# Feed-forward products by one level of Strassen's algorithm, and the gated products through DRAM to a separate output stage

## The chip, the cores and the metric

The kernel runs on one core of a Trainium2 chip. The metric is device time in microseconds: the median of the runs, from the start of the execution to its end. A core has a matrix engine (TensorE; "PE" in the profile, with its weight loads as "PEld"), three engines for elementwise work (VectorE "DVE", ScalarE "ACT", GpSimd "POOL"), and queues that issue transfers (SyncE "SP" here for nearly all loads, POOL's queue for stores). The matrix engine reads the on-chip SBUF and writes the accumulator memory PSUM, of 8 banks with 512 four-byte columns each, on 128 partitions.

## The reference

One inference step of a small two-layer backbone on 1152 tokens (128 context tokens and 1024 latent tokens), model width 1024. Layer 0 mixes tokens by retention and pooling, layer 1 by attention. After each mixer comes a feed-forward block, and this is what the change is about:

```python
def swiglu(h, w_in, w_out):
    a, b = jnp.split(h @ w_in, 2, axis=-1)
    return (jax.nn.silu(a) * b) @ w_out

fs = swiglu(rmsnorm(xs, norm_gain[i, 2]) * (1.0 + sc2s) + sh2s, w_ffn_in[i], w_ffn_out[i])
xs = xs + g2s * rmsnorm(fs, norm_gain[i, 3])
```

`w_in` is 1024 x 5632 (2816 gate columns `a`, 2816 value columns `b`), `w_out` is 2816 x 1024. The same is done for the context tokens with their own shift, scale and gate. sc2, sh2 and g2 come from a modulation that multiplies silu(c) with a 1024 x 6144 matrix per layer.

## The kernel before, in words

Everything is float32. A product that must keep its precision is made of three single-pass matmuls on the reduced type `F32R`: each operand is split into a rounded high part and the residue, and hi x hi, hi x lo and lo x hi are summed in PSUM (`mm3`, line 177). `split` makes the pair: a cast on ScalarE (line 154), a subtraction on VectorE (line 155).

Tokens are 9 tiles of 128 (`NT`), in 3 groups of 384 (`NG`, `GT`). `O` holds the residual tokens' normed values token by token; `hsteps` transposes them on TensorE (line 246), applies shift and scale on ScalarE (line 249) and splits into `h_hi` and `h_lo` in the large buffer `RR` (lines 251, 252). These steps are put into a list `later`, and `go(n)` issues n of them between matmul groups.

`out_proj` is the projection at the end of a mixer, by token tile; the last two tiles hold back part of their matmuls, between which the first group of `hsteps` is issued. `chain` is the norm with residual behind a tile's projection or feed-forward output: a sum of squares on ScalarE (217), 1/sqrt on GpSimd (182, 183), gain and residual on VectorE (229, 230), a store of the residual from POOL's queue, a second sum of squares (233), and a scale (235).

`ffn` runs over 11 pairs of 128-column tiles of the 2816 columns (`NPAIR`). In a pair, `A(p, g)` makes the gate and value product of a token group: per tile, 24 matmuls of 384 columns for the gate and 24 for the value (8 row tiles of the weights x 3 passes), then Silu on ScalarE (791), a product on VectorE (792) and a split. `B(p, g)` multiplies the result with two row tiles of `w_out`: 18 groups of 6 matmuls of 512 columns a pair, each added into `O` by VectorE (816; the first pair is copied by ScalarE, 814). The loads of the next pair's weights go through two staging buffers `RAW` and are split. In layer 0's block, `hook()` issues small units of the next layer's modulation (`Ada`): a load of 512 KB, four multiply-adds on VectorE (333), and from time to time a pair of matmuls with a ones column (316).

The order of the work is that of the program; the tile framework then sets the order on each engine by priorities and by when an instruction is ready, and adds the semaphores. Loads queue on SP in that order.

## Time and profile before

| what | value |
|---|---|
| median of 3 runs | 3002.43 us (3002.17 to 3002.64) |
| profiled execution, span | 2999.9 us; its own total is not recorded beside the span |
| busy: PE, DVE, ACT, POOL | 98%, 50%, 30%, 9% of the span |
| moved by DMA | 205.18 MB, mean 68 GB/s |
| layer 0's feed-forward block | about 692 to 1565 us, layer 1's about 2156 us to the end |

A row of a group view names line, engine, operation, tiles written and read, shape and count, then busy time and mean length of one in ns, then the idle time before such instructions and what ended it. A matmul's length in the profile includes its passage through the array, so that matmuls overlap; how often they start tells what they cost. L177 is a line of `mm3`, which every split product shares; the tiles and shapes tell them apart: in the feed-forward block `PS<-RR` with 128x384 is the first product, and `PS<-MID2True,MID1True` with 128x512 the second.

### The profile page before, as it was taken

The page shows a single profiled execution, that of the slowest core. Times are in us where ns is not written, and L with a number is a line of the kernel's source. Part 1 is how long each engine was busy: PE and PEld are TensorE (multiplying, and loading weights), DVE is VectorE, ACT ScalarE, POOL GpSimd, SP SyncE. Part 2 cuts the span into 40 slices and gives each one's busy share as a digit, 9 for nine tenths or more (in the row PEclk, how much of TensorE's full clock was granted, in tenths as well). Part 3 has the DMA queues.
Part 4 walks back from the last instruction along what each step waited for, and adds up shares of the span by engine and source line. Part 5 has one row for each costly group of instructions (what it writes and reads, how often), then busy time and mean ns, then how long its engine had stood idle before and what let it go on. Part 6 is the DMA issues. An engine that isn't in the chain of part 4 may idle for free. (4 is left out here: it accounts for less than half of the span.)

```text
span 2999.9 us, 40862 instructions
## 1 busy us (share of the span) xinstructions
PE 2949.6 (98%) x16907; PEld 2659.8 (89%) x16907; DVE 1502.4 (50%) x2483; ACT 910.5 (30%) x1678; POOL 279.7 (9%) x497
## 2 busy tenths in 40 slices
PE   7999999999999999999999999999999999999998
PEld 4889998789888888999989988888899999999997
DVE  5783346436455554333375567885523333333335
ACT  5222223324211111111153467874431111111112
POOL 2010112110000000000034621110100000000001
PEclk9999999999999999999999999999999999999999
DMA  7531110413333332111131000002311111111112
GB/s 242 170 105 48 34 32 33 149 59 97 92 99 99 99 99 85 43 43 43 43 128 61 22 15 1 29 29 85 127 43 43 43 43 43 43 43 43 43 43 99
DMA packets 169396, 205.18 MB, mean 68 GB/s; under 512 B 7085, under 2 KB 126313, under 8 KB 169081
## 3 DMA queue, kind: packets, MB, share of 16 engines
q1 hardware_dynamic: 163968, 186.67, 19.8%
q0 software_dynamic: 4752, 15.52, 1.3%
q8 instruction: 132, 2.16, 0.3%
q14 instruction: 56, 0.45, 0.0%
q10 hardware_dynamic: 488, 0.38, 0.0%
HBM read 182.33 MB, written 20.22 MB: 68 GB/s over the span
## 5 line engine op out<-in xcount | busy, mean ns | idle before, releaser
L177 PE MATMUL PS<-RR 128*128 128x384 f32 (+2 forms) x10800 | 1805.9, 324 | 3.4 <-DVE O L229 1.9
L177 PEld LDWEIGHTS PS<-RR 128*128 128x128 f32 x10800 | 1717.1, 189 | 49.9 <-issue 19.0
L177 PE MATMUL PS<-MID2True,MID1True 128*128 128x512 f32 x2376 | 568.2, 396 | 0.5 <-DVE O L816 0.5
L177 PEld LDWEIGHTS PS<-MID2True,MID1True 128*128 128x128 f32 x2376 | 443.8, 188 | 109.9 <-issue 4.2
L792 DVE TENSOR_TENSOR XGT<-XGT,PS 128x384 f32<-128x384 f32 x132 | 73.1, 554 | 553.5 <-PE PS L177 551.5
L816 DVE TENSOR_TENSOR O<-PS,O 128x512 f32<-128x512 f32 x360 | 245.7, 689 | 165.3 <-PE PS L177 164.8
L155 DVE TENSOR_TENSOR RR<-RAW,RR 128x1024 fp32r<-128x1024 f32 (+1 forms) x141 | 172.8, 1230 | 232.1 <-ACT RR L154 208.8
L177 PE MATMUL PS<-RR,MID2True 128*128 128x256 f32 (+1 forms) x1464 | 280.5, 340 | 0.3 <-DVE MID2True L155 0.2
L154 ACT CAST RR<-RAW 128x1024 fp32r<-128x1024 f32 (+1 forms) x141 | 147.0, 1047 | 409.6 <-PE PS L177 389.8
L177 PEld LDWEIGHTS PS<-RR,MID2True 128*128 128x128 f32 x1464 | 226.8, 189 | 32.6 <-DVE MID2True L155 0.7
L182 POOL TENSOR_SCALAR SM<-SM 128x1 f32<-128x1 f32 (+1 forms) x153 | 56.6, 370 | 1655.0 <-ACT RR L217 1178.5
L154 ACT CAST MID1True<-XGT 128x384 fp32r<-128x384 f32 x132 | 67.6, 512 | 376.2 <-DVE XGT L792 376.1
L177 PE MATMUL PS<-MID1True,RR 128*128 128x512 f32 (+1 forms) x576 | 145.2, 369 | 2.2 <-ACT XGT L1032 1.7
L791 ACT ACTIVATE XGT<-PS 128x384 f32<-128x384 f32 x132 | 64.5, 489 | 243.1 <-PE PS L177 238.8
L333 DVE SCALAR_TENSOR_TENSOR XGT<-XGT,PW 128x512 f32<-128x512 f32 x168 | 117.3, 747 | 17.7 <-ACT XGT L331 12.3
L1030 DVE TENSOR_REDUCE SM<-PS 128x1 f32<-128x1280 f32 x64 | 95.4, 1491 | 41.6 <-PE PS L177 41.1
L154 ACT CAST RR<-PS 128x512 fp32r<-128x512 f32 x160 | 93.6, 586 | 64.0 <-PE PS L1048 62.9
L154 ACT CAST MID2True<-RAW 128x1024 fp32r<-128x1024 f32 x44 | 44.2, 1046 | 221.0 <-PE PS L177 220.7
L177 PEld LDWEIGHTS PS<-MID1True,RR 128*128 128x128 f32 x576 | 92.4, 189 | 15.4 <-ACT XGT L1032 2.6
L183 POOL TENSOR_TENSOR SM<-SM,PW 128x1 f32<-128x1 f32 (+1 forms) x153 | 103.8, 679 | 12.4
L155 DVE TENSOR_TENSOR RR<-PS,RR 128x512 fp32r<-128x512 f32 x160 | 103.8, 682 | 1.3 <-ACT RR L154 1.3
L1048 PE MATMUL PS<-CT,XGT 128*128 128x128 f32 x640 | 98.6, 276 | 0.7 <-DVE RR L155 0.7
(208 smaller groups left out, 1936.8 us busy)
## 6 DMA issues: line engine op xcount, KB each, us to landing
RAW<-in_w_ffn_in_dram SPq DMA_DIRECT2D x88, 512.0 KB
XGT<-in_w_ada_dram SPq DMA_DIRECT2D x54, 512.0 KB
RAW<-in_w_ffn_out_dram SPq DMA_DIRECT2D x44, 512.0 KB
O<-in_w_ada_dram SPq DMA_DIRECT2D x32, 512.0 KB
RAW<-in_w_in_even_dram SPq DMA_DIRECT2D x28, 512.0 KB
x<-XGT POOLq DMA_DIRECT2D x27, 512.0 KB, 3.0
XGT<-x SPq DMA_DIRECT2D x23, 512.0 KB
RAW<-in_w_out_even_dram SPq DMA_DIRECT2D x12, 512.0 KB
```

Of the source, the lines that this page charges most:

```text
L154: nc.scalar.copy(hi, src)
L155: nc.vector.tensor_sub(lo, src, hi)
L177: nc.tensor.matmul(out=out, lhsT=x, rhs=y, start=(first and c == 0), stop=(last and c == n - 1))
L182: nc.gpsimd.tensor_scalar(r, ss, 1.0 / n, EPS, op0=ALU.mult, op1=ALU.add)
L183: nc.gpsimd.tensor_tensor(r, r, nhalf[:, 0:w], op=ALU.pow)
L333: nc.vector.scalar_tensor_tensor(self.acc[kind], b[:, k], sv, self.acc[kind], op0=ALU.mult, op1=ALU.add)
L791: nc.scalar.activation(tm, pss[0], ACTF.Silu)
L792: nc.vector.tensor_mul(tm, tm, pss[1])
L816: nc.vector.tensor_add(dst, p3, dst)
L1030: nc.vector.reduce_max(nm, sp, axis=AX.X, negate=True)
L1048: nc.tensor.transpose(tp[:, c:c + 128], smx[n, e][:, j * 128:(j + 1) * 128], ident)
```

## The change

The first product is done by Strassen's algorithm in Winograd's form, one level deep: the tokens are cut into two halves of 576, the 1024 model columns into two halves of 512, and the output columns into gate and value. With X the normed tokens and A the weights of one 128-column tile f (`a11`, `a12` for the gate, `a21`, `a22` for the value), four sums of weight blocks and five sums of token blocks (three of them sums proper, and the plain second half counted in) enter seven block products P1 to P7, where the plain way has eight. Each block product is 12 matmuls over 192 token columns and 12 over 384 (`product`, line 829). `prep` splits one weight block or sum for the product three steps on; the sums are made on GpSimd (`sums`, 809). `after` takes a product from PSUM and adds it on: the first half of the tokens' gate is P1 + P2 in PSUM, the other parts are built on VectorE from u2 and u3 (858 to 871). The gated product of a tile, 128 x 1152, is stored to DRAM (`gg_scr`).

The token sums need all nine tiles. `first_half` makes the operands of P1 and P2 during the held-back matmuls of `out_proj`; `second_half` makes the rest beside eight P1 and P2 products of the first four tiles (`NPRO`), which go ahead of the loop.

The second product is a stage of its own after all 22 tiles (`output`): chunks of 2, 4, 3, 4, 2, 3, 4 tiles (`NCH`), for each of which the gated products come back from DRAM through one staging buffer (`gr`) and are split, and 18 groups of 6 matmuls per tile run; VectorE adds into `O` once a chunk. In the last chunk the norm chain of each token tile starts when the tile is done. `chain` became a generator so that its steps can be laid between others. The modulation units go to two places of the loop and of the output stage, and with `shared` they add their row right away, because their PSUM bank is also a product's.

```diff
-        def A(p, g, fs=range(2)):
-            for f in fs:
-                pss = []
-                for ab in range(2):
-                    hi, lo = (x.rearrange("p (k f) -> p k f", k=KD) for x in w_unit(2 * f + ab))
-                    ps = bank(ab if abank["n"] % 2 == 0 else 2 + ab)[:, 0:GT]
-                    mm3(ps, [(hi[:, k], lo[:, k], h_hi(g)[:, k], h_lo(g)[:, k]) for k in range(KD)])
...
+    PROD = {P1: ("a", 0, 0, 0), P6: ("s", 1, 3, 1), P7: ("s", 2, 4, 2), P5: ("s", 0, 2, 3),
+            P2: ("a", 1, 1, 0), P4: ("a", 3, 5, 2), P3: ("s", 3, 6, 3)}
+            pro = [(0, P1), (1, P1), (0, P2), (1, P2), (2, P1), (3, P1), (2, P2), (3, P2)]
+            self.steps = pro + [(f, p) for f in range(NF)
+                                for p in ((P6, P7, P5, P4, P3) if f < NPRO else (P1, P6, P7, P5, P2, P4, P3))]
...
+        def sums(self, f):
+            nc.gpsimd.tensor_tensor(s[0], a21, a22, op=ALU.add)
+            nc.gpsimd.tensor_tensor(s[1], s[0], a11, op=ALU.subtract)
+            nc.gpsimd.tensor_tensor(s[2], a11, a21, op=ALU.subtract)
+            nc.gpsimd.tensor_tensor(s[3], a12, s[1], op=ALU.subtract)
...
+        def product(self, s):
+            for c0, w, o in ((0, 192, 320), (192, 384, 512)):
+                ps = PS[:, 1024 * reg + o:1024 * reg + o + w]
+                for k in range(4):
+                    ks = slice(128 * k, 128 * k + 128)
+                    xh, xl = self.xop(x, k, 0, c0, w), self.xop(x, k, 1, c0, w)
+                    for u, v in ((wh, xh), (wh, xl), (wl, xh)):
+                        nc.tensor.matmul(out=ps, lhsT=u[:, ks], rhs=v, start=first and n == 0, stop=n == 11,
...
+        def second_half(self, j, b):
+                    nc.tensor.transpose(ps[:, i * 128:(i + 1) * 128], O[:, k, t * 128:(t + 1) * 128], ident)
+                self.evac_h(k, ps[:, p0:p0 + w], tm, ((1, 0, w),))
+            nc.vector.tensor_sub(t1, x12, op(0, 0))
+            nc.vector.tensor_sub(t1, t1, op(0, 1))
+            nc.gpsimd.tensor_tensor(t3, x22, x12, op=ALU.subtract)
+            nc.scalar.copy(op(6, 0), x22)
+            nc.scalar.copy(op(2, 0), t1)
+            nc.vector.tensor_sub(t2, x22, t1)
+            nc.scalar.copy(op(3, 0), t2)
+            nc.vector.tensor_sub(op(2, 1), t1, op(2, 0))
+            nc.vector.tensor_sub(t4, op(1, 0), t2)
+            nc.vector.tensor_add(t4, t4, op(1, 1))
+            nc.scalar.copy(op(5, 0), t4)
+            nc.scalar.copy(op(4, 0), t3)
+            nc.vector.tensor_sub(op(3, 1), t2, op(3, 0))
+            nc.vector.tensor_sub(op(5, 1), t4, op(5, 0))
+            nc.gpsimd.tensor_tensor(op(6, 1), x22, op(6, 0), op=ALU.subtract)
+            nc.gpsimd.tensor_tensor(op(4, 1), t3, op(4, 0), op=ALU.subtract)
...
+        def out_prep(self, f):
+            gh, gl, wh, wl = self.out_slot(f)
+            gr = XGT[:, 4096:5248]
+            nc.sync.dma_start(out=gr, in_=gg_scr[self.l][f])
+            w = raw()
+            nc.sync.dma_start(out=w, in_=a["w_ffn_out"][self.l, f * 128:(f + 1) * 128, :])
+            split(gh, gl, gr)
+            for h in range(2):
+                split(wh[h], wl[h], w[:, 512 * h:512 * h + 512])
...
+            for ci, nf in enumerate(NCH):
+                for t in range(NT):
+                    for half in range(2):
+                        mm3(ps, items)
+                        if ci == 0:
+                            nc.scalar.copy(dst, p3)
+                        else:
+                            nc.vector.tensor_add(dst, p3, dst)
+                        if todo and n % every == 0:
+                            self.out_prep(todo.pop(0))
```

Three places where the order of instructions differs. First TensorE at the end of layer 0's mixer and the start of its feed-forward block. Rows name line, operation, output and inputs, shape and count; L246 and, after, L891 and L910 are transposes. Before:

```order
L246 MATMUL PS<-CT,O 128x128 x3
L177 MATMUL PS<-RR,MID2True 128x512 x24
L246 MATMUL PS<-CT,O 128x128 x12
L177 MATMUL PS<-RR 128x384 x56
L246 MATMUL PS<-CT,O 128x128 x6
L177 MATMUL PS<-RR 128x384 x16
```

And after, the same place:

```order
L891 MATMUL PS<-CT,O 128x128 x4
L179 MATMUL PS<-RR,MID2True 128x512 x24
L910 MATMUL PS<-CT,O 128x128 x4
L843 MATMUL PS<-RR 128x192 x12
L843 MATMUL PS<-RR 128x384 x12
L910 MATMUL PS<-CT,O 128x128 x6
```

Where transposes of the later groups lay between long runs of 384-column matmuls, there now stand four or six transposes of `second_half` ahead of each of eight products of 12 + 12.

Second TensorE in the middle of the block. Before, a pair:

```order
L177 MATMUL PS<-RR 128x384 x96
L177 MATMUL PS<-MID2True,MID1True 128x512 x24
L316 MATMUL PS<-XGT,PW 32x512 x2
L177 MATMUL PS<-MID2True,MID1True 128x512 x48
L177 MATMUL PS<-RR 128x384 x192
```

After, from a product on plain `RR` operands to the end of an f-tile's seven (P4 reads `MID1True`, P3 `MID2True` and two blocks elsewhere):

```order
L843 MATMUL PS<-RR 128x192 x12
L843 MATMUL PS<-RR 128x384 x12
L843 MATMUL PS<-MID1True,RR 128x192 x12
L843 MATMUL PS<-MID1True,RR 128x384 x12
L843 MATMUL PS<-MID2True,RR 128x192 x10
L843 MATMUL PS<-MID1True,RR 128x192
L843 MATMUL PS<-MID2True,RR 128x192
```

The 512-column matmuls have left the loop, and each run of 12 has its own weight loads.

Third ScalarE beside the first products. Before:

```order
L249 ACTIVATE XGT<-PS,modT,SC 128x384 x2
L154 CAST MID1True<-XGT 128x384
L249 ACTIVATE XGT<-PS,modT,SC 128x384 x6
L791 ACTIVATE XGT<-PS 128x384
L154 CAST MID1True<-XGT 128x384
```

After, one step of `second_half` over 384 columns with what follows it (L916 to L924 are its casts, L156 a weight block's, L856 takes P1 from PSUM):

```order
L883 ACTIVATE XGT<-PS,modT,SC 128x384 x2
L916 CAST MID2True<-XGT 128x384
L924 CAST RR<-XGT 128x384
L917 CAST RR<-XGT 128x384
L919 CAST RR<-XGT 128x384
L923 CAST MID1True<-XGT 128x384
L156 CAST RR<-RAW 128x512
L856 COPY O<-PS 128x576
```

Two evacuations became two and five casts a step, with the cast that needs GpSimd's difference (L924) ahead of three that don't.

More of the change, by code (lines that the diff above doesn't have):

```diff
@@ L23 @@
 DFF = 2816
-NPAIR = 11
+NF = 22
+NPRO = 4
+NCH = (2, 4, 3, 4, 2, 3, 4)
 SCALE = 128.0 ** -0.5
@@ L191, in hybrid_step_kernel @@
     x_scr = [[drp.tile([128, D], F32, name=f"x{s}_{t}") for t in range(NT)] for s in range(3)]
+    gg_scr = [[drp.tile([128, NT * 128], F32, name=f"gg{l}_{f}") for f in range(NF)] for l in range(2)]
     g_scr = [[[drp.tile([1, D], F32, name=f"g{l}_{s}_{k}") for k in range(2)] for s in range(2)] for l in range(2)]
@@ L205, in load_gates, with chain_steps @@
             nc.sync.dma_start(out=GB[k], in_=g_scr[l][s][k][0:1, :].broadcast_to([128, D]))
-    def chain(t, src, xs, xd, junk, last=False):
+    def chain_steps(t, src, xs, xd, junk, last=False):
         if last:
@@ L234, in chain @@
         r2 = rstd_of(s2, D)
+        yield
         nc.vector.tensor_scalar(ot, x3, r2, None, op0=ALU.mult)
+    def chain(*args, **kw):
+        for _ in chain_steps(*args, **kw):
+            pass
     later = []
@@ L314, in unit @@
             if kk == 0 and n:
+                rs = slice(32 * j - 32, 32 * j)
                 for kind in range(2):
-                    nc.tensor.matmul(out=bank(self.bk)[32 * j - 32:32 * j, :], lhsT=ones[:, kind], rhs=self.acc[kind],
+                    nc.tensor.matmul(out=bank(self.bk)[rs, :], lhsT=ones[:, kind], rhs=self.acc[kind],
                                      start=(kind == 0), stop=(kind == 1), tile_position=(0, 32 * j - 32))
+                if self.shared:
+                    nc.vector.tensor_add(self.brow[rs, :], bank(self.bk)[rs, :], self.brow[rs, :])
             if n == 16:
                 self.n = 17
-                ada_finish(l, i, self.brow, self.grow, self.bk)
+                ada_finish(l, i, self.brow, self.grow, self.bk, self.shared)
                 return
@@ L442, in hybrid_step_kernel, with ada_bufs @@
     hstage(0, 0, [3, 4, 5, 6])
+    def ada_bufs(buf):
+        return [buf[:, 1024 * x:1024 * x + 1024].rearrange("p (k c) -> p k c", k=2) for x in range(2)] + \
+            [buf[:, 2048 + 512 * x:2560 + 512 * x] for x in range(4)]
     adabufs = O[:, 2:6].rearrange("p k t -> p (k t)")
@@ L716, in fin @@
         def fin(t):
-            chain(t, bank(2 * (t % 2), 2), xs(t), xd(t), tok(t))
+            return chain_steps(t, bank(2 * (t % 2), 2), xs(t), xd(t), tok(t))
         for t in range(NT - 2):
@@ L721, in out_proj @@
             mms(t, cs, order, True, True)
-            fin(t)
+            for _ in fin(t):
+                pass
         c7, c8 = do_split(NT - 2), do_split(NT - 1)
+        if mid:
+            mid()
         mms(NT - 2, c7, late, True, False)
         mms(NT - 1, c8, late, True, False)
-        after_weights(False)
+        F.begin()
         rest = [k for k in order if k not in late]
-        hsteps(0, sub, [4, 5, 6, 7])
+        per = -(-16 // (4 * -(-len(rest) // 2)))
         for n in range(0, len(rest), 2):
-            mms(NT - 2, c7, rest[n:n + 2], False, n + 2 >= len(rest), 1)
@@ L731, in out_proj @@
-        after_weights(True)
-        fin(NT - 2)
+            mms(NT - 2, c7, rest[n:n + 2], False, n + 2 >= len(rest), per)
+        for _ in fin(NT - 2):
+            pass
+        F.prep(1)
+        F.prep(2)
         for n in range(0, len(rest), 2):
-            mms(NT - 1, c8, rest[n:n + 2], False, n + 2 >= len(rest), 1)
+            mms(NT - 1, c8, rest[n:n + 2], False, n + 2 >= len(rest), per)
         go()
-        fin(NT - 1)
-        hsteps(1, sub, [4, 5, 6, 7])
-    ffn_w = {}
-    def ffn_units(l, p, which):
-        wi = a["w_ffn_in"][l].rearrange("(k p) f -> p k f", p=128)
-        for i in which:
-            if i < 4:
-                f = 2 * p + i // 2
-                c0 = (DFF if i % 2 else 0) + f * 128
-                load_unit(wi[:, :, c0:c0 + 128], w_unit(i), k=8)
-            else:
-                f = 2 * p + i - 4
-                load_unit(a["w_ffn_out"][l, f * 128:(f + 1) * 128, :], w_unit(i))
+        F.tail = fin(NT - 1)
@@ L858, in hybrid_step_kernel @@
-    M1 = open_mid1(F32R)
-    nc.gpsimd.memset(XG[:, 2048:3072], 0.0)
-    for i in range(3):
-        adaq.append(Ada(1, i, XG, 6))
     wqkv = a["w_qkv"][0].rearrange("(k p) f -> p k f", p=128)
@@ L1122, in hybrid_step_kernel @@
     load_gates(1, 0)
[L1123 to L1126 removed]
+    F = FFN(1, M1, lambda t: x_scr[2][t], x_out, None)
+    out_proj(F, units, [0, 1, 2, 3, 4, 5, 6, 7], [0, 1, 2, 3, 4], lambda t: [(tok(t), 0, 8)],
+             lambda t: x_scr[1][t], lambda t: x_scr[2][t],
+             lambda t: [(M2[:, 0:1024], M2[:, 1024:2048]) if t % 2 else (M1[:, 0:1024], M1[:, 1024:2048])])
+    F.run()
     pool1.pop("cm").__exit__(None, None, None)
```

322 lines of the change are left out of this document (233 added, 89 removed).

## The prediction

> **What bounds the kernel now.** I read the engine totals first, then the timeline of TensorE inside a feed-forward stage, then the groups by shape, and last what TensorE waited for. The totals say that TensorE is the limit all through, at full clock:
>
> ```profile
> span 2999.9 us, 40862 instructions
> PE 2949.6 (98%) x16907; PEld 2659.8 (89%) x16907; DVE 1502.4 (50%) x2483; ACT 910.5 (30%) x1678; POOL 279.7 (9%) x497
> PEclk9999999999999999999999999999999999999999
> ```
>
> So time is won only by fewer or shorter matmuls, and lost wherever TensorE must now wait. The median of the runs, 3002.4 us, is 2.5 us over this span; I keep those 2.5 us as they are.
>
> Busy time of pipelined matmuls overlaps, so I take prices from start to start. In the timeline of TensorE in layer 1 and at the start of the attention projection, the columns are start, length, engine, line, operation, tiles, shape and count:
>
> ```profile
> 2204.02 16.81 PE L177 MATMUL PS<-RR 128*128 128x384 f32 x96
> 2220.68 16.96 PE L177 MATMUL PS<-MID2True,MID1True 128*128 128x512 f32 x72
> 2237.48 33.45 PE L177 MATMUL PS<-RR 128*128 128x384 f32 x192
> 2270.77 8.56 PE L177 MATMUL PS<-MID2True,MID1True 128*128 128x512 f32 x36
> ...
> 1565.73 7.91 PE L177 MATMUL PS<-RR 128*128 128x256 f32 x64
> 1573.47 0.38 PE L246 MATMUL PS<-CT,O 128*128 128x128 f32 x2
> ```
>
> A 384-column matmul costs (2270.77-2237.48)/192 = 173.4 ns, a 512-column one (2237.48-2220.68)/72 = 233.3 ns, a 256-column one (1573.47-1565.73)/64 = 120.9 ns. From 256 to 384 that is 0.41 ns a column.
>
> **The change, part by part.**
>
> *The products.* Before, the gate and value columns take 22 f-tiles x 2 x 3 token groups x 24 = 3168 matmuls of 384 columns a layer, 6336 in all. Now each f-tile has seven products of 12 matmuls over 192 columns and 12 over 384: 44 x 84 = 3696 of each width. The output matmuls stay 2376 of 512 columns. Columns streamed fall by an eighth, but half of the new matmuls are 192 wide, and no row of this trace has a matmul of that type and width. Drawing the 256-to-384 line on to 192 gives 120.9 - 64 x 0.41 = 94.7 ns, the low bound. The high bound is the 256-column row itself, 120.9 ns. Between them decides whether the weights arrive in time: each matmul has its own load of 128 columns, which hides behind the matmul ahead. Where a load started late, the trace shows its length. Two views of layer 0's output projection, weight loads first, then matmuls:
>
> ```profile
> 553.75 0.19 PEld L177 LDWEIGHTS PS<-RR,MID2True 128*128 128x128 f32 x1 [0.20 <-DVE RR L155]
> 553.86 0.19 PEld L177 LDWEIGHTS PS<-RR,MID2True 128*128 128x128 f32 x1
> 557.53 0.19 PEld L177 LDWEIGHTS PS<-RR,MID2True 128*128 128x128 f32 x1 [0.20 <-DVE RR L155]
> 557.64 0.19 PEld L177 LDWEIGHTS PS<-RR,MID2True 128*128 128x128 f32 x1
> ```
>
> ```profile
> 557.60 0.43 PE L177 MATMUL PS<-RR,MID2True 128*128 128x512 f32 x1
> 557.87 0.40 PE L177 MATMUL PS<-RR,MID2True 128*128 128x512 f32 x1
> ```
>
> The load at 557.53 had waited for VectorE. Its matmul is stamped 557.60 but is 0.03 us longer than its neighbour, and the one after it starts 0.23 us (one 512-column matmul) behind 557.64: it really began at 557.64, 0.11 us after its load, and only then did the next load begin. The pair at 553.75 and 553.86 shows the same 0.11. So loads follow one another at 0.11 us, and a matmul shorter than that waits for its weights. I take 109 ns for 192 columns, since these rows show the very thing that would limit it. The Trainium skill, "TensorE: Matmul & The Clock Gate", section "LDWEIGHTS (loading the stationary operand)", gives columns/1.2 ns, 106.7 ns for 128 columns; the trace agrees with its 0.11. By 106.7 the sum would be 8 us lower.
>
> Before: 6336 x 173.4 = 1098.7 us. After: 3696 x (173.4 + 109) = 1043.7 us. **-55.0 us.** An ideal eighth would be 137 us; the weight loads eat the rest.
>
> The same page, section "What overlaps and what doesn't", says that a load overlaps a running matmul only where the row groups differ. By that rule a 384-column matmul would cost 160 + 107 = 267 ns; the trace's 173.4 disagrees, so I give it no chance.
>
> *The way into the products.* Durations for the other engines, from the groups by shape (count, then busy us and mean ns):
>
> ```profile
> L249 ACT ACTIVATE XGT<-PS,modT,SC 128x384 f32<-128x384 f32 x64 | 40.0, 669 | 33.4 <-PE PS L246 21.2 <-DVE RR L252 10.9 <-PE PS L177 1.1
> L249 ACT ACTIVATE XGT<-PS,modT,SC 128x256 f32<-128x256 f32 x32 | 18.1, 567 | 0.0
> L249 ACT ACTIVATE XGT<-PS,modT,SC 128x128 f32<-128x128 f32 x32 | 14.8, 461 | 12.1 <-PE PS L246 8.8 <-ACT XGT L249 1.6 <-DVE RR L252 1.2
> L154 ACT CAST MID1True<-XGT 128x384 fp32r<-128x384 f32 x132 | 67.6, 512 | 376.2 <-DVE XGT L792 376.1
> L154 ACT CAST MID2True<-MID1False 128x512 fp32r<-128x512 f32 x9 | 5.6, 622 | 13.2 <-PE PS L177 13.1
> L814 ACT COPY O<-PS 128x512 f32<-128x512 f32 x36 | 21.1, 587 | 25.3 <-PE PS L177 25.0
> L217 ACT ACTIVATE O<-PS 128x1024 f32<-128x1024 f32 x18 | 18.4, 1022 | 3.1 <-PE PS L177 3.1
> L155 DVE TENSOR_TENSOR MID1True<-XGT,MID1True 128x384 fp32r<-128x384 f32 x132 | 73.4, 556 | 48.7 <-ACT MID1True L154 48.7
> L251 DVE CAST RR<-XGT 128x384 fp32r<-128x384 f32 x96 | 33.3, 358 | 23.1 <-ACT XGT L249 22.5
> L155 DVE TENSOR_TENSOR RR<-PS,RR 128x512 fp32r<-128x512 f32 x160 | 103.8, 682 | 1.3 <-ACT RR L154 1.3
> L816 DVE TENSOR_TENSOR O<-PS,O 128x512 f32<-128x512 f32 x360 | 245.7, 689 | 165.3 <-PE PS L177 164.8
> L1020 POOL TENSOR_TENSOR RR<-O,RR 128x256 fp32r<-128x256 f32 x32 | 23.9, 747 | 2.6
> L932 POOL TENSOR_TENSOR XGT<-XGT 128x256 f32<-128x256 f32 x35 | 33.6, 959 | 23.3 <-DVE XGT L923 23.2
> ```
>
> Strassen needs five token sums, all ready before the first P6, P7, P5, P4 and P3; eight P1 and P2 products are meant to cover their making. ScalarE, per layer. Ahead of the products: the first half's 8 evacuations of 384 (461+567 each) and 8 of 192 (halfway between 461 and 567, 514), 12.3 us; 3 weight casts, 1.9; the norm chain of tile 7, two passes of about 1.02 plus their readouts, 2.5. Beside the eight products: second half, 4 x (2 x 514 + 5 casts of 192 at about 350, by the 384 and 512 rows) = 11.1 and 4 x (2 x 669 + 5 x 512) = 15.6; tile 8's chain 2.5; 8 weight casts 5.0; 8 evacuations of 576 at about 650, 5.2. Total 16.7 + 39.4 = 56 us. VectorE comes to about the same: eight subtractions a step at 355 and 556, casts at 358, eleven weight residues at 682, two chains: 55 us. TensorE over the same stretch: the held-back matmuls of tiles 7 and 8, 72 (layer 0) or 36 (layer 1) x 0.233 = 16.8 or 8.4; 80 transposes at 0.10 (row below), 8; products 8 x 12 x 0.282 = 27.1. That is 52 and 43.5 us.
>
> ```profile
> 2180.48 1.14 PE L246 MATMUL PS<-CT,O 128*128 128x128 f32 x9
> 2181.38 0.78 PE L177 MATMUL PS<-RR 128*128 128x384 f32 x3
> ```
>
> So TensorE outruns its feeders by 4 and 12.5 us. ScalarE's cast of t3 also stands behind a GpSimd subtraction, and what waits behind that cast are the evacuations that TensorE's next transposes need; a 256-column GpSimd row takes 0.75 to 0.96, and I add half a microsecond of such hopping for each of eight steps, 4 us a layer. **+24.5 us**; +4 (everything overlaps, layer 0's slack serves) and +45 (all hops exposed) are the ends. The sums of the weights on GpSimd, four of 512 columns per f-tile, would take 1.5 to 1.9 us each in proportion to those rows; the first use needs two of them, and has two products (6.8 us) from their start. Should that cover go, each f-tile pays about 1 us.
>
> *Inside the loop* an f-tile takes 84 x 0.282 = 23.7 us. VectorE has 7 x 0.68 + 7 x 0.76 = 10 us, with layer 0's modulation sums 16; ScalarE 6.5. Evacuations have two or more products before their PSUM region is rewritten. Cost nothing, except where a modulation unit is issued one product before the ones-matmul that reads it: about 1 us, eight times in layer 0, less what the old hooks cost: **+3**. 16 more transposes: **+1.6**.
>
> *The output stage* does the same 2376 matmuls. VectorE loses 144 adds, which were hidden, and gains nothing on the path. Each f-tile now brings 590 KB back through one staging buffer. The nearest row is the store of a 512 KB tile:
>
> ```profile
> x<-XGT POOLq DMA_DIRECT2D x27, 512.0 KB, 3.0
> ```
>
> About 4.5 us with the issue, then 1.2 (cast) and 1.4 (subtract) before the buffer is free: 7 us, against 54 x 0.233 = 12.6 us of matmuls for an f-tile. Hidden, except in the first chunk, where two f-tiles (25.2 us) cover four loads (28 us): **+2 a layer, +4**; ends 0 and 12.
>
> *The way out of layer 0.* What TensorE waits for there now, from 1450 to 1620 us (us in total, times, longest), and VectorE's chain:
>
> ```profile
> PE PS L246 <- DVE O L235: 4.6, 6, 1.7
> PE PS L246 <- ACT XGT L249: 1.4, 2, 1.0
> PE PS L177 <- ACT XGT L909: 0.9, 1, 0.9
> ```
>
> ```profile
> L229 DVE SCALAR_TENSOR_TENSOR O<-O,SM,XGT 128x1024 f32<-128x1024 f32 x9 | 11.5, 1282 | 1.6 <-POOL SM L183 1.5
> L230 DVE TENSOR_TENSOR XGT<-O,XGT 128x1024 f32<-128x1024 f32 x27 | 32.8, 1222 | 0.5
> L235 DVE TENSOR_SCALAR O<-XGT,SM 128x1024 f32<-128x1024 f32 x27 | 20.3, 753 | 38.7 <-POOL SM L183 38.7
> ```
>
> Norm chains now start tile by tile through the last chunk (52 us) instead of three at a time, so transposes wait less: **-4**, ends -7 and +5 (VectorE has 18 x 0.69 = 12.4 of adds, 9 x 3.26 = 29 of chains and 24 x 0.91 = 22 of splits there, 64 us with nothing between them, and two thirds of the last chain and splits fall behind the projection's first matmuls). The end of the kernel keeps its last chain: 0.
>
> Sum: -55.0 + 24.5 + 3 + 1.6 + 4 - 4 = -26 us. 2999.9 - 26 + 2.5 = **2976 us**.
>
> **The rivals.**
> 1. *Weight loads hide after all*: 94.7 ns for 192 columns. 3696 x 14.3 = 53 us less: 2923. For it: the straight line through the wider rows. Against: the 0.11 us rows. The Trainium skill (same page, "Back-to-back issue gap") has columns/2.4 + 2.5 = 82.5 ns for an isolated stream; no run here shows it.
> 2. *A floor at the 256-column price*: the matmul needs its load plus the 12 ns or so by which the 256-column row exceeds the load. 120.9 ns: 3696 x 11.9 = 44 us more: 3020, **slower**. With my other terms it decides from 109 + 26/3.696 = 116 ns on.
> 3. *The feeders cost double*: token sums and hops expose 45 us, the first chunk 12: 2976 + 20 + 8 = 3004, no change.
> 4. *Below 256 columns the single pass is lost*, and 192 columns run like plain four-byte matmuls, which here are two records each:
>
> ```profile
> L546 PE MATMUL PS<-MID2False,O 128*128 128x512 f32 x32 | 16.7, 602 | 0.2 <-DVE MID2False L580 0.2
> ```
>
> 16 matmuls in 16.7 us is 2.0 ns a column, 0.39 us for 192: 3696 x 0.28 = over 1000 us more, about 4010. For it: only that the trace has no such width; nothing speaks directly.
>
> **How the numbers follow.** Mine 0.70 (own range 2950 to 3000), rival one 0.09, two 0.10, three 0.07, four 0.04. The range 2923 to 3020 takes in the first three rivals at their own prices, and leaves out the fourth and the tails. Of mine nearly all, rival one and a little of three are faster by over 0.2% (6 us, about what this kernel's runs can tell from nothing): 0.79; the same 0.05; slower 0.16.
>
> **What would show it.** The start-to-start time of the 192-column rows (109, or 95, or 121) decides most. Then TensorE's idle time around the first eight products of each layer, with the releaser named as ScalarE or VectorE, larger in layer 1; no idle time in the loop; small waits in the first output chunk. I am wrong if the 192-column price is off by 7 ns, or if TensorE idles more than some 50 us at the entrances.

## The result, and the profile after

The changed kernel takes 3033.95 us, median of 4 runs (3032.21 to 3034.96); the kernel before, run beside it on the same chip, 3002.3 us (3001.31 to 3002.64). The ratio is 1.0105, with a 95% interval from 1.0091 to 1.0119: 1% slower, where 2976 us (2923 to 3020) had been forecast. The profiled execution spans 3032.7 us, 32.8 more than before. Span, engines and granted clock:

```profile
span 3032.7 us, 44867 instructions
PE 2927.0 (97%) x17979; PEld 2640.9 (87%) x17979; DVE 1763.9 (58%) x2793; ACT 1047.3 (35%) x1950; POOL 581.1 (19%) x766
PEclk9999999999999999999999999999989999999999
```

TensorE still looks full, but its busy time fell by only 22.6 us while the span grew: it now waits. The waits of TensorE name the places; first the start of layer 0's feed-forward block (672 to 763 us), then of layer 1's (2144 to 2250), then the first output chunk of layer 0 (1265 to 1310) and of layer 1 (2734 to 2775); the columns are total, times, longest:

```profile
PE PS L843 <- ACT O L856: 7.4, 4, 4.2
PE PS L843 <- ACT O L864: 5.1, 1, 5.1
PE PS L843 <- DVE RR L925: 1.3, 1, 1.3
...
PE PS L843 <- ACT O L856: 8.0, 4, 3.3
PE PS L843 <- ACT O L864: 7.1, 2, 5.1
...
PE PS L179 <- ACT O L1038: 12.5, 2, 10.5
...
PE PS L179 <- ACT O L1038: 9.2, 1, 9.2
```

In the loop itself there is no wait: the same view from 763.4 to 1265 us is empty. The loop's price is read from a long window of layer 1 (columns: time, then busy us and count for PE, weight loads, DVE, ACT, POOL, then clock, DMA share, GB/s), and the two widths from the starts at the end of a P3 in layer 0:

```profile
2300.00:2700.00 400.00, 400.00 (x2794) 400.00 (x2792) 177.22 (x232) 101.69 (x167) 95.79 (x84) 1.00 0.21 68
```

```profile
1262.24 1.26 PE L843 MATMUL PS<-MID2True,RR 128*128 128x192 f32 x10
1263.34 0.27 PE L843 MATMUL PS<-MID1True,RR 128*128 128x192 f32 x1
1263.45 2.06 PE L843 MATMUL PS<-MID2True,RR 128*128 128x192 f32 x11
1265.35 0.34 PE L843 MATMUL PS<-RR 128*128 128x384 f32 x1
```

400/2794 is 143.2 ns a matmul, 286.4 a pair. Ten 192-column matmuls start in 1263.34 - 1262.24, 110 ns each; one more of them and ten of 384 columns take 1265.35 - 1263.45, which leaves 179 ns for 384. Such start times shift at each change of width: behind the start of a 192-column matmul the next weight load begins some 22 ns later, behind a 384-column one 3 ns later. By the starts of the weight loads, over the whole of layer 1's loop, the two widths cost 111 and 175 ns.

I measure two stretches by start times throughout. The *entrance* runs from the first held-back projection matmul to the start of the 14th product (eight ahead of the loop, five of f-tile 0):

```profile
672.26 1.55 PE L179 MATMUL PS<-RR 128*128 128x512 f32 x6
...
763.34 4.91 PE L843 MATMUL PS<-RR 128*128 128x192 f32 x36
...
2159.79 1.56 PE L179 MATMUL PS<-RR,MID2True 128*128 128x512 f32 x6
...
2249.64 3.59 PE L843 MATMUL PS<-RR 128*128 128x192 f32 x24
```

It takes 91.1 and 89.9 us. TensorE's own work there, at the unhindered prices (projection 16.8 or 8.4, 80 transposes 8, 13 products 44), is 68.9 and 60.5: 22 and 29 us are lost. The *first output chunk* runs from its first 512-column matmul through its 108: 41.5 us in layer 0 and 36.5 in layer 1, where 108 x 0.2333 is 25.2: 16 and 11 us are lost.

### The profile page after: what moved, and what is told of

It is laid out like the page before. It is cut to its first block, busy times and chain, and to the rows that moved or that the text cites. A ratio compares the mean times of both kernels' runs of the same rounds, so it can differ in the third digit from the quotient of the medians.

```text
span 3032.7 us, 44867 instructions
## 1 busy us (share of the span) xinstructions
PE 2927.0 (97%) x17979; PEld 2640.9 (87%) x17979; DVE 1763.9 (58%) x2793; ACT 1047.3 (35%) x1950; POOL 581.1 (19%) x766
## 5 line engine op out<-in xcount | busy, mean ns | idle before, releaser
L179 PE MATMUL PS<-RR 128*128 128x256 f32 (+2 forms) x6000 | 1068.5, 332 | 22.8 <-ACT O L1038 21.8
L843 PE MATMUL PS<-RR 128*128 128x192 f32 (+1 forms) x5324 | 797.6, 309 | 30.8 <-ACT O L856 15.3
L156 ACT CAST RR<-O 128x512 fp32r<-128x512 f32 (+1 forms) x242 | 151.8, 627 | 566.2 <-PE PS L843 415.7
L179 PE MATMUL PS<-RR,MID2True 128*128 128x512 f32 (+1 forms) x1524 | 312.0, 343 | 0.1
L156 ACT CAST RR<-RAW 128x512 fp32r<-128x512 f32 (+1 forms) x187 | 135.7, 738 | 397.6 <-PE PS L179 152.6
L157 DVE TENSOR_TENSOR RR<-RAW,RR 128x512 fp32r<-128x512 f32 (+1 forms) x187 | 157.9, 857 | 148.8 <-ACT RR L156 125.6
L157 DVE TENSOR_TENSOR RR<-O,RR 128x512 fp32r<-128x512 f32 (+1 forms) x242 | 173.0, 715 | 63.4 <-ACT RR L156 63.1
L345 DVE SCALAR_TENSOR_TENSOR O<-O,PW 128x512 f32<-128x512 f32 x224 | 161.0, 765 | 24.8 <-DMA O<-in_w_ada_dram 13.7
L843 PE MATMUL PS<-MID1True,RR 128*128 128x192 f32 (+1 forms) x1100 | 170.4, 305 | 0.0
L843 PEld LDWEIGHTS PS<-MID1True,RR 128*128 128x128 f32 x1100 | 160.4, 190 | 0.0
L843 PE MATMUL PS<-MID2True,RR 128*128 128x192 f32 (+1 forms) x968 | 158.7, 307 | 0.0
L156 ACT CAST RR<-PS 128x512 fp32r<-128x512 f32 x160 | 93.6, 586 | 64.7 <-PE PS L1272 63.5
L179 PEld LDWEIGHTS PS<-MID1True,RR 128*128 128x128 f32 x576 | 92.5, 189 | 15.3 <-ACT XGT L1256 2.6
L157 DVE TENSOR_TENSOR RR<-PS,RR 128x512 fp32r<-128x512 f32 x160 | 103.9, 681 | 3.2 <-ACT RR L156 3.0
```

The lines of the kernel that those rows point to most:

```text
L156: nc.scalar.copy(hi, src)
L157: nc.vector.tensor_sub(lo, src, hi)
L179: nc.tensor.matmul(out=out, lhsT=x, rhs=y, start=(first and c == 0), stop=(last and c == n - 1))
L345: nc.vector.scalar_tensor_tensor(self.acc[kind], b[:, k], sv, self.acc[kind], op0=ALU.mult, op1=ALU.add)
L843: nc.tensor.matmul(out=ps, lhsT=u[:, ks], rhs=v, start=first and n == 0, stop=n == 11, skip_group_check=not first)
```

## The experiments

All edits are against the changed kernel, unless said otherwise.

| kernel | median us | ratio to before, 95% |
|---|---|---|
| changed kernel | 3033.95 | 1.0091 to 1.0119 |
| e1 two blocks of 288 columns | 2934.32 | 0.9759 to 0.9788 |
| e2 token sums on VectorE | 3019.68 | 1.0040 to 1.0073 |
| e3 three staging buffers | 3022.61 | 1.0051 to 1.0081 |
| e4 192 and 384 alternating | 3035.29 | 1.0093 to 1.0123 |
| e5 e1, e2 and e3 together | 2917.31 | 0.9701 to 0.9733 |
| e6 e5, PSUM read first | 2919.77 | 0.9711 to 0.9740 |
| e7 added transposes, shared bank | 3056.10 | 1.0162 to 1.0192 |
| e8 e5, first weight sums on VectorE | 2914.96 | 0.9691 to 0.9724 |
| e9 each early P1 made twice | 3032.56 | 1.0083 to 1.0113 |
| e10 added transposes, own bank | 3035.09 | 1.0091 to 1.0121 |
| e11 three banks for transposes | 3036.61 | 1.0093 to 1.0123 |
| e12 e8, a fifth f-tile ahead | 2909.29 | 0.9674 to 0.9707 |

**e1. Two blocks of 288 columns**

```diff
-            for c0, w, o in ((0, 192, 320), (192, 384, 512)):
+            for c0, w, o in ((0, 288, 224), (288, 288, 512)):
```

> Each block product runs over two token blocks of 288 columns instead of 192 and 384; nothing else of the order changes (the operand block that was in two places gets one place, and half a weight slot moves to make room). Theory A (a short matmul waits for its own weight load, so 192 columns pay the load's 0.11 us and 288 columns do not): the line from 256 columns (120.9 ns) to 384 (173.4 ns) gives 134 ns for 288, a pair 268 ns where the changed kernel's loop has 286.4. 3696 pairs x 18.4 ns = 68 us less than the changed kernel: 2966 us, 36 us faster than the kernel before. Rival B (the pair of blocks has a fixed price, two blocks of 576 columns in sum cost some 283 to 286 ns however they are cut): no change, 3034 us.

2934.32 us: 99.6 less than the changed kernel, more than Theory A gave. The window of layer 1's loop:

```profile
2250.00:2600.00 350.00, 350.00 (x2643) 350.00 (x2642) 166.71 (x220) 95.49 (x156) 88.66 (x78) 1.00 0.23 73
```

350/2643 is 132.4 ns a matmul, 265 a pair where 192 + 384 cost 286.4. So the length of a block decides, not the pair: the short half had been bound by its weight load, and 288 columns cost about what the line from 256 to 384 gives (134 ns). The two loops give 73.4 of the 100 us, the entrances 6.7. The other 21 came unasked, in the first output chunk (30.7 and 26.3 us). There the framework put ScalarE's instructions into another order. The changed kernel's ScalarE first, then e1's:

```profile
1271.22 1.15 ACT L156 CAST MID1True<-XGT 128x1152 fp32r<-128x1152 f32 x1 [4.83 <-DMA XGT<-gg]
1272.28 1.13 ACT L156 CAST MID1True<-RAW 128x512 fp32r<-128x512 f32 x2
1277.74 1.15 ACT L156 CAST MID2True<-XGT 128x1152 fp32r<-128x1152 f32 x1 [4.32 <-DMA XGT<-gg]
...
1281.57 1.54 ACT L1038 COPY O<-PS 128x512 f32<-128x512 f32 x3
```

```profile
1229.48 0.58 ACT L1038 COPY O<-PS 128x512 f32<-128x512 f32 x1
...
1234.31 1.16 ACT L156 CAST MID1True<-XGT 128x1152 fp32r<-128x1152 f32 x1 [1.20 <-DMA XGT<-gg]
```

In the changed kernel the casts of the gated products for the *second* chunk (`MID1True`, `MID2True`) stand ahead of the first chunk's copies from PSUM, and each waits over 4 us for its load; TensorE, with all four banks full, waits 10.5 us for the first copy. In e1 the copy comes first. It has one staging buffer just the same and loses 5.5 and 1.1 us there instead of 16 and 11, so the place in ScalarE's queue seems to be most of the loss; no run changes that order alone.

**e2. Token sums on VectorE**

```diff
-            nc.gpsimd.tensor_tensor(t3, x22, x12, op=ALU.subtract)
+            nc.vector.tensor_sub(t3, x22, x12)
...
-            nc.gpsimd.tensor_tensor(op(6, 1), x22, op(6, 0), op=ALU.subtract)
-            nc.gpsimd.tensor_tensor(op(4, 1), t3, op(4, 0), op=ALU.subtract)
+            nc.vector.tensor_sub(op(6, 1), x22, op(6, 0))
+            nc.vector.tensor_sub(op(4, 1), t3, op(4, 0))
```

> The three subtractions that each step of second_half has on GpSimd go to VectorE: 12 of 192 columns (about 0.355 us) and 12 of 384 (0.556 us) a layer, 10.9 us more of VectorE work a layer, and 25 us or so of GpSimd work less. Theory A (a VectorE operation on SBUF that starts beside a GpSimd operation does not end before it; the two engines' times add up, 55 + 27 us beside 52 and 43.5 us of TensorE): the two entrances, 91.1 us in layer 0 and 89.9 in layer 1 with some 22 and 29 us lost, get shorter by 5 to 14 us each; VectorE's 192- and 384-column subtractions return to 0.36 and 0.56 us; total about 3015 us (3005 to 3025). Rival B (the two engines work side by side, VectorE is simply the fuller engine): entrances longer by about 11 us each, total about 3055 us. Rival C (the loss is the hops from engine to engine and ScalarE's own 56 us): within 4 us of the changed kernel, 3030 to 3038.

3019.68 us; the entrances fell to 85.5 and 78.7 us, by 5.6 and 11.2, although VectorE got 24 operations more a layer. VectorE was busy for less time with more work: 67.2 and 66.6 us at the entrances instead of 72.9 and 71.8. This is Theory A. GpSimd and then VectorE in the changed kernel, over the same 5 us:

```profile
717.68 1.33 POOL L927 TENSOR_TENSOR MID2True<-XGT,MID2True 128x384 fp32r<-128x384 f32 x1
718.97 1.32 POOL L928 TENSOR_TENSOR RR<-XGT,RR 128x384 fp32r<-128x384 f32 x1
720.25 1.58 POOL L813 TENSOR_TENSOR O<-O,RAW 128x512 f32<-128x512 f32 x1
```

```profile
718.24 1.19 DVE L918 TENSOR_TENSOR XGT<-XGT 128x384 f32<-128x384 f32 x1
719.46 1.24 DVE L921 TENSOR_TENSOR XGT<-RR,XGT 128x384 f32<-128x384 f32 x1
720.63 1.61 DVE L920 TENSOR_TENSOR RR<-XGT,RR 128x384 fp32r<-128x384 f32 x1
```

Each VectorE operation ends 0.4 us after one on GpSimd (719.43 after 719.01, 720.70 after 720.29, 722.24 after 721.83) and takes 1.2 to 1.6 us. The same lines by shape, layer 0's entrance, the changed kernel and then e2:

```profile
L921 DVE TENSOR_TENSOR XGT<-RR,XGT 128x384 f32<-128x384 f32 x4 | 5.0, 1248 | 0.1
```

```profile
L921 DVE TENSOR_TENSOR XGT<-RR,XGT 128x384 f32<-128x384 f32 x4 | 2.2, 547 | 0.0
```

1248 ns beside GpSimd, 547 without. The Trainium skill, "SBUF — State Buffer", section "Who interferes with whom", says that a VectorE instruction with two SBUF inputs contends with a GpSimd instruction that reads SBUF, that the port pair they share is an exclusive lock, and that the order of issue decides who is blocked; the trace agrees. What the run does not separate: it also spares ScalarE's casts the wait for GpSimd's differences, so a part of the 16.8 us may be such hops from engine to engine.

**e3. Three staging buffers**

```diff
-            gr = XGT[:, 4096:5248]
+            gr = (XGT[:, 4096:5248], RR[:, 9216:10368].bitcast(F32), RR[:, 10368:11520].bitcast(F32))[(f ^ 1 if f < 2 else f) % 3]
```

> The gated products that come back from DRAM rotate through three staging buffers (the old one and two that lie where the operand of P6 was, free after the last P6) instead of one. Theory A (the single buffer: each load waits until VectorE has read the one before, and the casts that wait for it stand on ScalarE ahead of the copies that free PSUM for the first output chunk): the first chunk falls from 41.5 us in layer 0 and 36.5 in layer 1 to 25 to 27 us, 24 to 27 us less in all: about 3009 us. Rival B (ScalarE and VectorE are full there whatever the loads do: casts, residues, and in layer 0 fourteen multiply-adds of the modulation): layer 1 gains at most 5 us, layer 0 nothing: 3029 us or more.

3022.61 us; the first chunks fell from 41.5 and 36.5 us to 31.9 and 29.2, 16.9 us of the 27.6 lost. The whole run gained only 11.3 us: in this trace the stretches ahead of the two blocks, which the edit doesn't touch, took 6 us longer, and why is not known. The result lies between the two theories: the single buffer was a cause, and what is late next shows on ScalarE, the output weights through the two `RAW` buffers (which no run changes alone):

```profile
1273.79 1.14 ACT L156 CAST MID1True<-RAW 128x512 fp32r<-128x512 f32 x2 [1.64 <-DMA RAW<-in_w_ffn_out_dram]
1274.84 1.16 ACT L156 CAST MID2True<-RR 128x1152 fp32r<-128x1152 f32 x1
1278.58 1.14 ACT L156 CAST MID2True<-RAW 128x512 fp32r<-128x512 f32 x2 [2.58 <-DMA RAW<-in_w_ffn_out_dram]
```

**e4. Alternating widths.** The loop over the two blocks goes inside the loop over the 12 weight loads.

> The 12 matmuls of 192 columns and the 12 of 384 of a block product alternate, each pair with the same weights (loaded twice as before), instead of 12 and then 12. Theory A (one weight load ahead: a matmul can start its load only when the one before has begun, so each 192-column matmul holds up its successor to 0.11 us wherever it stands): a pair stays at 282 to 286 ns, total 3034 us, plus or minus 5. Rival B (loads run further ahead, so a long matmul pays for a short one): a pair costs 173.4 + 94.7 = 268 ns, 3696 x 18.4 = 68 us less, 2966 us.

3035.29 us; a long window of layer 1's loop gives 390/2738 = 142.4 ns a matmul:

```profile
2310.00:2700.00 390.00, 390.00 (x2738) 390.00 (x2737) 173.24 (x229) 99.19 (x163) 91.74 (x81) 1.00 0.22 69
```

Theory A. A pair costs 285 ns where it cost 286.4, so a long matmul doesn't pay for its short neighbour. The starts of the matmuls alone would say otherwise (88 ns behind a short one, 197 behind a long one); by the starts of the weight loads it is 108 and 177, close to the 111 and 175 of the changed kernel.

**e5. The first three edits together**

> The three edits together: two blocks of 288 columns, the token sums of second_half on VectorE alone, three staging buffers for the gated products. If the three act on separate places, the savings add up: from the 288-column kernel's 2934.3 us the entrances give back 12 us (5.6 in layer 0 and 11.2 in layer 1 were measured with 192 and 384 columns, less what the 288-column kernel's different order already took), and the first output chunk 4 to 6 us (30.7 and 26.3 us there, 25.2 without a wait): 2917 us (2908 to 2926). Rival (shorter products give the feeders less cover, and VectorE, the fuller engine, decides at the entrance): the entrances stay at 85 to 89 us, total 2928 to 2935 us.

2917.31 us, as the sum had it (2917). The first chunks take 25.3 and 25.5 us, so nothing is lost there any more. The entrances, 84.2 and 79.3 us with shorter products, still lose some 18 and 22. TensorE's longest waits there, 7.1 and 7.3 us, are for a weight residue on VectorE (L157). Late there too are the four weight sums of f-tile 0, on GpSimd (in layer 1):

```profile
2130.50 14.83 POOL L812 TENSOR_TENSOR O<-RAW 128x512 f32<-128x512 f32 x1 [2.31 <-PE PS L910]
2145.41 1.26 POOL L813 TENSOR_TENSOR O<-O,RAW 128x512 f32<-128x512 f32 x1
```

The first sum takes 14.83 us, the second of the same size 1.26. VectorE ran without a gap until 2144.2, and then had to wait itself, through ScalarE:

```profile
2146.70 0.62 ACT L156 CAST RR<-O 128x512 fp32r<-128x512 f32 x1 [4.17 <-POOL O L813]
...
2148.18 0.56 DVE L920 TENSOR_TENSOR RR<-XGT,RR 128x384 fp32r<-128x384 f32 x1 [3.98 <-ACT RR L917]
```

**e6. e5, and a product is read from PSUM ahead of the next token sums.** `self.after(s)` moves ahead of `self.second_half(...)`. In this kernel the copy of f-tile 1's P1 overwrites 64 columns of `O` that the third step still has to read; the work is the same.

> As the kernel with the three edits, and beside the first eight products the reading of a product from PSUM is issued ahead of the next step's token sums instead of behind them. Theory A (what TensorE waits for at the entrance is the ScalarE copy that frees its PSUM region, and that copy stands behind five casts which wait for VectorE): the waits of products on the ScalarE copies of P1 and P2, 10.9 and 6.8 us with 192 and 384 columns, go to under 3 us a layer, 5 to 12 us less in all. Rival B (ScalarE and VectorE have that much work, 56 and 66 us a layer by my count, against 50 and 41.5 us of TensorE; the wait only moves to the transposes or to the operand of P6): within 4 us of the kernel with the three edits.

2919.77 us: Rival B. The waits on the P1 and P2 copies, 4.2 and 5.4 us in e5, are 4.6 and 6.0. The copy's place in the order was not the cause of the wait.

**e7. Added transposes, first try**

```diff
+            for n in range(12 if 0 < s < 9 else 0):
+                nc.tensor.transpose(PS[:, 896:1024], ident, ident)
```

They overwrite 128 columns of the last token tile's projection.

> The changed kernel with 12 more transposes of the identity, into unused PSUM columns, ahead of each of the second to ninth products of a layer: 192 in all, 0.10 us each, 9.6 us a layer, which need nothing and so run while TensorE would wait. Theory A (after a wait TensorE runs at half clock for some microseconds, which costs the entrances 7.0 and 9.3 us beside 14.8 and 19.8 us of waiting): the granted clock of the entrances, 0.93 and 0.90, rises above 0.97, the slow matmuls go from some 16 us to under 5, most of the added transposes fall into waits: total 3022 to 3034 us although 19 us of work are added. Rival B (the slow stretches have another cause, such as the traffic of the casts on PSUM): the clock stays, the slow matmuls stay, and what doesn't fit into waits is added: 3035 to 3050 us.

3056.10 us, and inconclusive: the added transposes share a bank with the products, and the framework made them wait for the same copies (waits of 15.4 and 15.8 us stand ahead of them), so they filled nothing. But they show the clock on work that reads no other engine's results. Twelve of them after a short wait, and after a long one:

```profile
721.02 1.53 PE L836 MATMUL PS<-CT 128*128 128x128 f32 x12 [0.22 <-ACT O L866]
...
738.93 2.82 PE L836 MATMUL PS<-CT 128*128 128x128 f32 x12 [6.91 <-ACT O L858]
```

**e8. e5, and the four weight sums of f-tile 0 on VectorE.** `sums(0)` is called with `nc.vector`.

> The kernel with the three edits, and the four weight sums of the first f-tile (512 columns each) go from GpSimd to VectorE too; those of the other 21 f-tiles stay on GpSimd. In the kernel with three edits the first of these sums lasted 13.7 us in layer 0 and 14.8 in layer 1 on GpSimd, where one takes 1.3 inside the loop: it ended when VectorE paused. ScalarE's cast of that sum waited 4.2 us for it in layer 1, with the casts that feed VectorE behind it. Theory A (GpSimd is shut out as long as VectorE's two-operand subtractions follow without a gap, and the stall comes from that): four sums cost VectorE 4 x 0.62 = 2.5 us, the 4 us stall and the half clock behind it (1.5 us) go: 2 to 4 us less a layer, 2911 us (2907 to 2914). Rival B (VectorE's own work sets the end of the entrance, the stall is only where the slack shows): 2.5 us more a layer, 2922 us.

2914.96 us, 2.35 less than e5, a step that the two intervals don't separate: the sign is Theory A's, the size not. The 14 us sum and the wait behind it are gone, and the entrances fall by 1.9 and 2.8 us to 82.2 and 76.5. Now Rival B's reason holds too. Windows of layer 0's entrance, the changed kernel and then e8:

```profile
710.00:720.00 10.00, 10.00 (x73) 9.62 (x71) 9.65 (x16) 7.38 (x17) 6.82 (x7) 1.00 0.27 79
720.00:730.00 10.00, 5.82 (x24) 5.64 (x23) 9.30 (x12) 4.55 (x9) 6.24 (x6) 0.67 0.18 52
730.00:740.00 10.00, 5.18 (x34) 4.59 (x32) 9.34 (x10) 4.56 (x9) 6.49 (x5) 0.98 0.28 80
```

```profile
710.00:720.00 10.00, 9.34 (x68) 8.45 (x66) 10.00 (x28) 9.50 (x23) 0.00 (x0) 1.00 0.27 81
720.00:730.00 10.00, 7.29 (x52) 6.82 (x52) 10.00 (x22) 8.31 (x17) 0.00 (x0) 1.00 0.28 78
730.00:740.00 10.00, 2.20 (x8) 1.96 (x8) 10.00 (x21) 4.36 (x8) 0.00 (x0) 0.66 0.01 2
```

VectorE (third pair of columns) is full in both. In the changed kernel it does 38 operations in 30 us, in e8 71. There it has no gap at all, and TensorE idles beside it, longest (8.6 us in each layer) for ScalarE's cast of the first weight sum, which VectorE has made just before, behind its token sums:

```profile
737.13 0.62 ACT L156 CAST RR<-O 128x512 fp32r<-128x512 f32 x1 [0.56 <-DVE O L812]
...
737.80 2.40 PE L843 MATMUL PS<-RR 128*128 128x288 f32 x8 [8.64 <-ACT RR L156]
```

So VectorE's own work, in its order, is the bound that is left in this stretch; no run takes work off it there.

**e9. Each early P1 made twice**

```diff
-            for c0, w, o in ((0, 192, 320), (192, 384, 512)):
+            for c0, w, o in ((0, 192, 320), (192, 384, 512)) * (2 if s < self.npro and p == P1 else 1):
```

> The changed kernel with each of the four P1 products that go ahead of the loop made twice in a row (the second pass writes the same result over the first): 96 matmuls or 13.6 us of TensorE work more a layer, and nothing more for any other engine. Theory A (at the entrance TensorE waits for feeders that have a fixed amount of work, so more products there are cover): most of the 13.6 us goes into waits of 14.8 and 19.8 us and into stretches at half clock: the entrances grow by 0 to 5 us each, total 3034 to 3044 us. Rival B (each step has its own chain of hops that starts only when the product before has ended): the entrances grow by 13 us each, total 3061 us.

3032.56 us. 27 us of TensorE work were added and nothing was lost: the entrances are 92.1 and 88.9 us, against 91.1 and 89.9. This is Theory A, and even a little under its 3034 to 3044 us: with 14 us more of TensorE work in each entrance, the feeders still set its length. So the 6.7 us that e1 won there do not simply come from its shorter products; from what, was not tried.

**e10. Added transposes in a bank of their own** (24 ahead of each of five products), and **e11**, its control.

```diff
+            for n in range(24 if 3 < s < 9 else 0):
+                nc.tensor.transpose(PS[:, 3968:4096], ident, ident)
...
-                ps = bank(4 + 2 * (j % 2) + n)
+                ps = bank(4 + (2 * (j + 4 * b) + n) % 3)
```

> The changed kernel with 24 transposes of the identity (0.10 us each) ahead of each of the fifth to ninth products of a layer, 120 a layer and 12 us, into a PSUM bank of their own, so that they wait for nothing; the transposes of second_half use three banks instead of four to free it. Theory A (after some 3 us without work TensorE runs at half clock for a while): the added work fills the waits of 3 to 5 us there, the granted clock of the entrances rises from 0.92 and 0.91 to above 0.96, slow matmuls fall from 16.3 us to under 6 in both layers, and the total is 3025 to 3037 us although 24 us of work are added. Rival B (the slow matmuls have another cause, for instance ScalarE and VectorE at the same PSUM): the slow matmuls stay at 14 us or more, total 3037 to 3050.

> Control for the kernel with the added transposes: the transposes of second_half rotate through three PSUM banks instead of four, nothing else is changed. If the fourth bank serves no purpose, within 4 us of the changed kernel's 3034; if the transposes then wait for ScalarE's evacuations, up to 10 us a layer more.

3035.09 and 3036.61 us. The control equals the changed kernel within its spread (3031.74 to 3037.49). The entrances of layers 0 and 1, of the changed kernel and then with the transposes:

```profile
672.00:763.00 91.00, 77.25 (x465) 71.50 (x464) 72.85 (x121) 49.75 (x109) 40.37 (x43) 0.92 0.22 67
2160.00:2250.00 90.00, 71.48 (x432) 66.15 (x431) 71.83 (x120) 50.28 (x110) 41.95 (x43) 0.91 0.22 67
```

```profile
674.00:765.00 91.00, 85.11 (x586) 79.24 (x586) 72.92 (x121) 50.05 (x110) 40.67 (x43) 1.00 0.22 68
2160.00:2248.00 88.00, 79.70 (x548) 75.39 (x547) 71.75 (x119) 50.11 (x109) 42.28 (x43) 0.96 0.22 69
```

The clock is 1.00 and 0.96 instead of 0.92 and 0.91. The matmuls that start 40 ns or more late, long waits left out, sum to 2.4 and 5.5 us instead of 7.0 and 9.3 (together 7.9, where under 6 had been expected). Theory A is right on the cause (half clock follows idle time) and the time fits it, but the entrances are 91.1 and 88.4 us, where the changed kernel has 91.1 and 89.9 and the control 92.7 and 88.4: with the clock nearly restored, 1.6 us at most is gained. The half clock lay in TensorE's slack, and the expectations of e7 and e8 had counted it as a cost.

**e12. e8, and P1 and P2 of a fifth f-tile ahead of the loop**

```diff
-NPRO = 4
+NPRO = 5
...
-            pro = [..., (2, P1), (3, P1), (2, P2), (3, P2)]
+            pro = [..., (2, P1), (3, P1), (2, P2), (4, P1), (3, P2), (4, P2)]
```

Its weights are staged in, and its results kept in, `XGT[:, 4096:5248]`; the load is issued after the third product. The weight sums of f-tile 0 and the splits behind them are issued one product later than in e8.

> The kernel with four edits, and the products P1 and P2 of a fifth f-tile go ahead of the loop too (10 products beside the token sums instead of 8; their weights and results lie in the part of XGT that the token sums leave free after their third step). The number of matmuls is the same; 48 of them, 6.4 us a layer, move from the loop to the entrance. Theory A (the end of the entrance is set by VectorE, which is busy without a gap from 710 to 740 us in layer 0, while TensorE has idle time there): the moved products fill TensorE's idle time, less two more weight residues on VectorE (1.2 us) and what the waits behind them cost: 3 to 6 us less a layer, 2905 us (2902 to 2910). Rival B (the cast of the fifth tile's weights waits on ScalarE for its load, which can start only when the third step of the token sums is over, and everything behind it waits too): no gain, 2913 to 2918 us.

2909.29 us, 5.7 less than e8, ratio to the kernel before 0.969 (0.9674 to 0.9707): the fastest of all, 3.1% faster than before. Of 12.7 us of products that were moved (four of 24 x 132.4 ns) about half lies in idle time now: the two loops together are 10.9 us shorter, and the entrances, with two more products each, grew by 3.0 and 3.5 us.

## Why the prediction was wrong, point by point

**The price of 192 columns** was right within 2 ns: 111 by the starts of the weight loads (110 by those of the matmuls) against 109, from two late weight loads. Rivals 1 (94.7) and 2 (120.9) are out, and rival 4 as well. The Trainium skill's load of 106.7 ns ("TensorE: Matmul & The Clock Gate", section "LDWEIGHTS (loading the stationary operand)") agrees with the 111 measured. What I did not see is its use: a split at 288 stays clear of that floor.

**The products' term (-55.0)** was a little mis-sized at both halves. A pair is 286.4 instead of 282.4 ns, so the term is 3696 x 0.2864 - 1098.7 = -40.2: some 2 ns more for 192 columns, and 175 instead of 173.4 for 384. (By the starts of the matmuls the 384 seem to cost 176.9 in the mean, because one in twelve, the first behind a run of 192, shows 200 ns; the interval at the other change of width, 88 ns, is as much too short.)

**The way into the products (+24.5, ends +4 and +45)** measured 22 + 29 = 51: the step that failed most. Place, releaser (ScalarE, behind its casts) and order (layer 1 worse) came out as said, though the waits stood ahead of products that needed the copies of P1 and P2, where I had named the transposes; that TensorE outruns its feeders is shown by e9. The size failed in the sentence that put ScalarE at 56 us and VectorE at 55 side by side with GpSimd: I counted GpSimd's operations only as half a microsecond of hop each. VectorE and GpSimd took turns, and taking GpSimd out of the token sums gave back about 17 of the 27 us too little (e2); the other 10 are not assigned to one cause. The hint was in the trace before, in a line of which I had quoted only the mean:

```profile
L932 POOL TENSOR_TENSOR XGT<-XGT x35: 727/975/1652, 1585.4 to 1728.5; 128x256 f32<-128x256 f32 x35
```

Shortest, median and longest of one GpSimd operation of one shape: the longest is 2.3 times the shortest, and I did not ask what it had been held up by. The same trace tells:

```profile
1655.11 1.21 DVE L155 TENSOR_TENSOR RR<-RAW,RR 128x1024 fp32r<-128x1024 f32 x1
1655.27 1.65 POOL L932 TENSOR_TENSOR XGT<-XGT 128x256 f32<-128x256 f32 x1 [0.72 <-DVE XGT L923]
```

This longest one began behind a VectorE subtraction with two SBUF inputs and ended 0.6 us after it. The ones near the median each began 0.04 us behind such a subtraction (L931) and also ended 0.6 us after it; beside those near 0.73 no such subtraction was under way at their start.

**The loop (+3)**: no wait in it, and 80 ones-matmuls before as after: 0. The weight sums on GpSimd stayed covered, as said.

**The output stage (+4, ends 0 and 12)** measured 16 + 11 = 27, beyond its upper end. The step that failed is "two f-tiles (25.2 us) cover four loads (28 us)": I compared sums of time, 25.2 against 28 us, and did not look at what stands *behind* a late load on its engine. The 7 us a load were right (casts at 1271.22 and 1277.74, 6.5 us apart). But the casts for the next chunk stood ahead of this chunk's copies, so waits that nobody needed became TensorE's. e1 and e3 each remove part of it, e5 all.

**The way out of layer 0 (-4)** did not come: TensorE's waits there are 5.0 + 2.8 + 0.4 = 8.2 us, against 7.4. **The end of the kernel (0)** costs 2.4: from the last matmul's start to the end 13.4 us instead of 11.0.

Summed from measured parts: -40.2 + 51 + 27 + 1 + 2.4 + 1.6 for the added transposes is +43 us, where the span grew by 32.8. About 3 of the 10 us between are output matmuls of layer 1, which start every 230.3 ns instead of 233.5 (the 1080 behind the first chunk), 2 are waits at the entrances of the kernel before (0.7 and 1.2 us); the rest is not assigned.

**The rivals.** Rival 3, feeders that cost double and a first chunk of 12 us, was nearest to what happened, and I gave it 0.07. Its price was too low, because I had taken my own upper ends for limits. The result lies outside my range because that range took the rivals one at a time, while the entrances, the first chunk and the products all came out dearer at once.

## What to carry to other kernels

When an algorithm saves matmuls, cut what is left so that no piece falls under the length of its weight load: the two loops lost 73 us (3384 pairs, 21.4 ns each) to a 192 + 384 split, which 288 + 288 gives back. Work that is moved to VectorE and GpSimd together is not shared between them where both read two SBUF operands: add their times. And for each load that may come late, ask what stands behind its first reader in that engine's queue. Idle time and a low clock on TensorE were symptoms here, and adding free work to the stretch (e9) tells within one run whether TensorE or its feeders set its length.

## What the runs showed of the hardware that I had not expected

- VectorE and GpSimd shut each other out where both read SBUF, in both directions: a 384-column VectorE subtraction took 1.25 us beside GpSimd instead of 0.55, and a GpSimd sum of 512 columns took 14.83 us instead of 1.26 while VectorE ran without a gap. Why they took turns in one kernel and GpSimd was shut out in the other is not shown.
- In the feed-forward blocks of all these runs the granted clock was half for 3.4 to 13.7 us around the end of each idle time of 4 us and more: 12 transposes took 2.82 us behind one of 6.91 us, and 1.53 behind one of 0.22. The Trainium skill, "TensorE: Matmul & The Clock Gate", section "What's actually happening", has half the clock after an idle window of about 3.4 us; the traces agree. In these entrances it cost next to nothing (e10).
- VectorE's subtractions follow one another more closely than their lengths say: in e5's gap-free stretch 0.27 us from start to start for 192 columns (length 0.35), 0.47 for 384 (0.55). My sums from lengths were too high by 17 to 30%, which will have hidden a part of the error.
